# Layer 0's softmax divides the output, not the probabilities; the sums travel with the meta tokens; v's transposes later

## The chip, the cores and the metric

The kernel runs on one core of one Trainium2 chip. The metric is the time of one execution on the device in microseconds, lower is better. The kernel before took 1788.43 us (median of three runs, 1787.76 to 1789.2).

A core has five engines with a queue of instructions each: TensorE (PE, with its weight loads shown as PEld), VectorE (DVE), ScalarE (ACT), GpSimd (POOL) and SyncE (SP, which here only issues DMA transfers). Each works through its queue in order; semaphores hold an instruction until what it needs is there. Matmuls write to PSUM, a small memory that DVE and ACT read; all else lies in SBUF or in DRAM.

## The reference, cut to what matters

An encoder of two layers over 512 tokens and 16 learned meta tokens (T = 528, width 2048). Layer 0 is attention with 16 query heads of 128 on 8 pairs of key and value heads, layer 1 gated linear attention. The change lies in layer 0:

```python
def _attend(qb, k, v):
    s = jnp.einsum('bqkgd,bskd->bkgqs', qb, k) * (ATTN_HEAD_DIM ** -0.5)
    p = jax.nn.softmax(s.astype(jnp.float32), axis=-1).astype(v.dtype)
    return jnp.einsum('bkgqs,bskd->bqkgd', p, v)

def attention_mixer(h, w_in, q_norm, k_norm, w_out, ang_row, ang_col):
    proj = h @ w_in
    q, k, v, gate = jnp.split(proj, ...)
    q = apply_axial_rope(rmsnorm(q, q_norm), ang_row, ang_col)
    k = apply_axial_rope(rmsnorm(k, k_norm), ang_row, ang_col)
    ...
    return (o * jax.nn.silu(gate)) @ w_out
```

## The kernel before

**Numbers as pairs.** A float32 matrix is held as a high and a low part (names ending in h and l, or hi and lo), each in the format that PE takes for one pass. A product is three matmuls: high by high, high by low, low by high. ACT makes the high part by a copy, DVE the low part by a subtraction. Every projection of the input (`project`) is a run of 16 such triples into a PSUM tile pp, L152 to L154, once for each half of the tokens (264 columns); weights come by DMA (wraw) and are split into whi and wlo.

**Layer 0, group by group.** A group g is one pair of key and value heads with its two query heads. While a group's attention runs, PE also computes the projections of the next group (k, two of q, then v) and of gates: the attention's matmuls stand between those of the projections. The stretch of these eight groups is about 213 to 751 us of the span.

The attention of a group has nine softmaxes, eight over 128 queries and one over the 32 queries of the meta tokens. Each goes through these steps:

- scores s on PE (L636 to L638, twice three matmuls) into the only PSUM buffer of s;
- their negative maximum mx on DVE (L641);
- the exponential on ACT into the tile pn, with the row sums sm (L644);
- on DVE, the reciprocal of sm (L645), then pn times it: 512 columns of real tokens (L646), and the 16 columns of the meta tokens, written three times with 32 columns between, into the tile's tail (L647);
- transposition on PE: four transposes pT (L654) and one of the tail, pTm (L656, 80 rows);
- ACT copies pT to ph and pTm to pmt (L658, L660); DVE forms the low parts pl and the last rows of pmt (L659, L661).

The three copies in the tail stand at rows 0, 32 and 64 of pTm, against the high, low and high part of the meta tokens' v in the tile vm: one matmul does the three products. Four times in a group `weighted` follows: 13 matmuls into the PSUM tile o (L674 to L677, 256 or 272 columns), and ACT's copy of o to o_sb (L678).

**v.** v's projection is transposed as it is needed with tokens in rows. ACT copies pp to vt in two halves (L576); then PE transposes, four times vps (L581) and once vpm for the meta tokens (L588); ACT scales each part of vps by its row factor into vh (L584), DVE forms vl (L585), and likewise for vm (L590 to L592). ACT and DVE take turns here on one PSUM tile. `values` sets when the transposes are written: `clk.after(1.2, late)`, 1.2 us behind the projection by the kernel's own clock.

**PSUM.** The tiles vps, vpm, pT and pTm share a pool of two buffers (ps_t). Each new one waits until the reader of the last but one is through.

**Gates.** Stored gates come back by DMA (gr, issued on SP at L610), are multiplied on DVE (L614), go through three exponentials and logarithms on ACT (L137 to L139) and a product on POOL (gs, L624); og = o_sb times gs on DVE (L618). There are two buffers of gr, so a load waits for the product gs two gates before. POOL also rotates q and k: L294 to L296 for each of the three projections of a group (k, and q twice), on their copies qw; its inputs qs come by DMA from L293.

**What sets the order.** The program writes instructions in an order driven by a small clock (`Clock`): each triple of projection matmuls moves it by its computed length, and pieces of attention put themselves in at due times with `clk.after`. A scheduler then orders each engine's queue from priorities in that order. So a piece that is due later stands later on PE, and shifts what ACT and DVE do for it.

Of the kernel before, what the change touches and what calls it, by code (L numbers as in the profile page):

```python
# [10 lines left out]
F32 = mybir.dt.float32  # L11
F32R = mybir.dt.float32r
I32 = mybir.dt.int32
AF = mybir.ActivationFunctionType
ALU = mybir.AluOpType
# [4 lines left out]
P = 128  # L20
D = 2048
KT = D // P
SEQ = 512
META = 16
T = SEQ + META
HALF = T // 2
# [56 lines left out]
def hybrid_encoder(  # L83
# [6 lines left out]
    V, A, G, PE = nc.vector, nc.scalar, nc.gpsimd, nc.tensor  # L90
    clk = Clock()

    def pool(stack, name, bufs=1, **kw):
        return stack.enter_context(tc.tile_pool(name=name, bufs=bufs, reuse_waits="tile", **kw))
# [17 lines left out]
    ident = const.tile([P, P], F32, name="ident")  # L112
    make_identity(nc, ident)
    ones = const.tile([P, P], F32, name="ones")
# [41 lines left out]
    def project(src, c0, parts, evac, last_k=None, ws=None):  # L156

        ws = ws or [weights(src[:, k0:k0 + 8, c0:c0 + P]) for k0 in (0, 8)]
        for a, b in parts:
            ps = ps_p.tile([P, 512], F32, tag="pp", name="pp")[:, :b - a]  # L160
            for k in range(KT):
                wh, wl = ws[k // 8]
                three(ps, wh[:, k % 8], wl[:, k % 8], k, a, b, k == 0, k == KT - 1)
                clk.step(3 * (b - a + 7) / 2400)
                if last_k and (a, b) == parts[-1]:
                    last_k(k)
            evac(ps, a, b)
# [169 lines left out]
    ps_t = pool(st, "ps_t", 2, space=PSUM)  # L337
# [44 lines left out]
    for i, (si, off) in enumerate(((0, 0), (1, 0), (1, P))):  # L382
        for j, (a, b) in enumerate(HALVES):
            n = 2 * i + j
# [117 lines left out]
    ps_t = pool(ps0, "ps_t0", 2, space=PSUM)  # L502
# [56 lines left out]
    pb = pool(l0, "pb0")  # L559
    wa = pool(l0, "wa0", 2)  # L560
    NP = 3
    REP = 80
    pn_bufs = [pb.tile([P, T + 96], F32, name=f"pn{i}") for i in range(NP)]
    for t in pn_bufs:
        G.memset(t, 0.0)
    vm_bufs = [pb.tile([REP, P], F32R, name=f"vm{i}") for i in range(2)]
    for t in vm_bufs:
        G.memset(t.bitcast(F32), 0.0)
    n_pn = [0]

    def values(g):
        vh = wa.tile([P, 4, P], F32R, tag="vh", name="vh")
        vl = wa.tile([P, 4, P], F32R, tag="vl", name="vl")
        vm = vm_bufs[g % 2]
        if g:
            project(w_in0, 3072 + g * P, HALVES, lambda ps, a, b: A.copy(vt[:, a:b], ps))  # L576

        def late():
            ps = ps_t.tile([P, 512], F32, tag="t", name="vps")
            for t in range(4):  # L580
                PE.transpose(ps[:, t * P:(t + 1) * P], vt[:, t * P:(t + 1) * P], ident)  # L581
            for t in range(4):
                pst = ps[:, t * P:(t + 1) * P]
                A.activation(vh[:, t, :], pst, AF.Copy, scale=rcol[:, t:t + 1])  # L584
                V.scalar_tensor_tensor(vl[:, t, :], pst, rcol[:, t:t + 1], vh[:, t, :].bitcast(F32),  # L585
                                       op0=ALU.mult, op1=ALU.subtract)
            pm = ps_t.tile([P, 512], F32, tag="t", name="vpm")[:META, :P]
            PE.transpose(pm, vt[:, SEQ:T], ident)  # L588
            rm = rcol[:META, 4:5]
            A.activation(vm[0:META], pm, AF.Copy, scale=rm)  # L590
            A.activation(vm[64:64 + META], pm, AF.Copy, scale=rm)
            V.scalar_tensor_tensor(vm[32:32 + META], pm, rm, vm[0:META].bitcast(F32),  # L592
                                   op0=ALU.mult, op1=ALU.subtract)
        clk.after(1.2 if g else 2.0, late)
        return vh, vl, vm

    def qkv(g):
# [35 lines left out]
    def softmax(n, qh, ql, kh, kl):  # L633
        s = ps_s.tile([P, 2, 512], F32, tag="s", name="s")[:n, :, :HALF]
        for i, (a, b) in enumerate(HALVES):
            PE.matmul(s[:, i], qh, kh[:, a:b], start=True, stop=False)  # L636
            PE.matmul(s[:, i], ql, kh[:, a:b], start=False, stop=False)  # L637
            PE.matmul(s[:, i], qh, kl[:, a:b], start=False, stop=True)  # L638
        mx = wa.tile([P, 1], F32, tag="mx", name="mx")[:n]
        sm = wa.tile([P, 1], F32, tag="sm", name="sm")[:n]  # L640
        V.reduce_max(mx, s, axis=AX.XY, negate=True)  # L641
        pn = pn_bufs[n_pn[0] % NP][:n]
        n_pn[0] += 1
        A.activation(pn[:, :T].rearrange("p (a b) -> p a b", a=2), s, AF.Exp, bias=mx, accum_out=sm)  # L644
        V.reciprocal(sm, sm)  # L645
        V.tensor_scalar(pn[:, :SEQ], pn[:, :SEQ], sm, None, op0=ALU.mult)  # L646
        V.tensor_scalar(pn[:, T:].rearrange("p (r m) -> p r m", r=3)[:, :, :META],  # L647
                        pn[:, SEQ:T].unsqueeze(1).broadcast_to([n, 3, META]), sm, None, op0=ALU.mult)
        return pn

    def transposed(pn, n, puts):
        pt = ps_t.tile([P, 512], F32, tag="t", name="pT").rearrange("p (t q) -> p t q", t=4)
        for t in range(4):
            PE.transpose(pt[:, t, :n], pn[:, t * P:(t + 1) * P], ident[:n, :n])  # L654
        pm = ps_t.tile([P, 512], F32, tag="t", name="pTm")[:REP]
        PE.transpose(pm[:, :n], pn[:, T:T + REP], ident[:n, :n])  # L656
        for (ph, pl, pmt), qc, c, m in puts:
            A.copy(ph[:, :, c:c + m], pt[:, :, qc:qc + m])  # L658
            V.tensor_tensor(pl[:, :, c:c + m], pt[:, :, qc:qc + m], ph[:, :, c:c + m].bitcast(F32), op=ALU.subtract)  # L659
            A.copy(pmt[:, c:c + m], pm[:, qc:qc + m])  # L660
            V.tensor_tensor(pmt[64:, c:c + m], pm[64:, qc:qc + m], pmt[64:, c:c + m].bitcast(F32), op=ALU.subtract)  # L661

    def p_tiles():
        ph = wa.tile([P, 4, 272], F32R, tag="ph", name="ph")
        pl = wa.tile([P, 4, 272], F32R, tag="pl", name="pl")
        pmt = wa.tile([REP, 272], F32R, tag="pmt", name="pmt")
        return ph, pl, pmt

    def weighted(pts, c, n, vv, o_sb):
        ph, pl, pmt = pts  # L670
        vh, vl, vm = vv
        o = ps_o.tile([P, 512], F32, tag="o", name="o")[:, :n]
        for t in range(4):
            PE.matmul(o, vh[:, t, :], ph[:, t, :n], start=(t == 0), stop=False)  # L674
            PE.matmul(o, vh[:, t, :], pl[:, t, :n], start=False, stop=False)
            PE.matmul(o, vl[:, t, :], ph[:, t, :n], start=False, stop=False)
        PE.matmul(o, vm, pmt[:, :n], start=False, stop=True)  # L677
        A.copy(o_sb[:, c:c + n], o)  # L678

    def attention(qk, vv, o_sb, slot):  # L680
        qh, ql, kh, kl = qk
        q0 = (0, Q1)
        todo = []
        for a in range(2):
            pts = [None]
            todo += [(P, q0[a] + t * P, [(pts, 0, t * P, P)], [(pts, 0, 256, a)] if t else [], t == 0)
                     for t in range(2)]
        late = [[None], [None]]
        todo.append((2 * META, SEQ, [(late[a], a * META, 256, META) for a in range(2)], [], True))
        for a in range(2):  # L690
            todo += [(P, q0[a] + 256 + t * P, [(late[a], 0, t * P, P)], [(late[a], 256, 272, a)] if t else [], False)
                     for t in range(2)]
        prev = None
        for item in todo + [None]:
            if item is not None:
                n, c, puts, ends, fresh = item
                pn = softmax(n, qh[:, c:c + n], ql[:, c:c + n], kh, kl)
            yield slot / 2
            if prev is not None:
                n_, _, puts_, ends_, fresh_ = prev[0]  # L700
                if fresh_:
                    for cell, *_ in puts_:
                        cell[0] = p_tiles()
                transposed(prev[1], n_, [(cell[0], qc, cc, m) for cell, qc, cc, m in puts_])
                for cell, cc, m, a in ends_:
                    clk.after(slot * 1.1, lambda cell=cell, cc=cc, m=m, a=a: weighted(cell[0], cc, m, vv, o_sb[a]))
            yield slot / 2
            prev = (item, pn) if item is not None else None
        yield 0.0

    def o_tiles():
        return [wa.tile([P, T], F32, tag="o", name="o_sb", bufs=4) for _ in range(2)]

    qk, vv = qks[0][0], values(0)
    held = None
    for g in range(KV):
        o_sb = o_tiles()
# [100 lines left out]
    ps_t = pool(tr, "ps_t1", space=PSUM)  # L818
# [145 lines left out]
    for a, b in HALVES:  # L964
        ps = ps_t.tile([P, 512], F32, tag="t", name="lrf")[:64, :b - a]
        PE.matmul(ps, fold, lt[:, a:b], start=True, stop=True)
        for d in range(2):
            pd, t = ps[d * 32:d * 32 + 16], lrs[d]
# [478 lines left out]
```

## Time and profile before

| | |
|---|---|
| median of three runs | 1788.43 us |
| span of the profiled execution | 1784.8 us |
| PE busy | 1753.4 us, 98% of the span |
| DVE, ACT, POOL busy | 1126.2, 951.4, 292.8 us |
| PE busy in the stretch 205 to 755 us | 538.07 of 550 us |
| DVE, ACT busy in it | 375.88, 315.23 us |

The profile shows no time around the span; the median of the runs lies 3.6 us above it. A group's row gives a line of the kernel, the engine, the operation, what it writes and reads, and how often; then busy time, the mean time of one in ns, and the time that the engine stood idle just before it with what ended that. A row of waits names the engine and tile that waited, the instruction waited for, the total, the count and the longest. A row of the timeline begins with the start from the span's start and the duration. Matmuls overlap: the distance between starts is what one costs PE.

### The profile page before, as it was taken

Reading aid. Unit: us, or ns where it says so; the run is one execution under the profiler, and the core shown is the slowest. Engines: PE = TensorE matmul, PEld = TensorE weight load, DVE = VectorE, ACT = ScalarE, POOL = GpSimd, SP = SyncE. Lnnn points to the kernel's source line nnn. Section 1 sums busy time; section 2 is a strip of 40 time slices with the busy share of each in tenths; the row PEclk is TensorE's granted clock in tenths of the full one; section 3 lists DMA queues with packets and bytes.
Section 4 is the critical chain, followed back from the end, with each engine's and each line's share of the span. In section 5 each row is a group of like instructions: output and inputs, shape, how many; then the busy total and the mean of one; then the engine's idle time right before and its main releaser. Section 6 shows DMA issues by size and latency. Waiting matters only on the chain.

```text
span 1784.8 us, 31606 instructions
## 1 busy us (share of the span) xinstructions
PE 1753.4 (98%) x12591; PEld 1653.0 (93%) x12591; DVE 1126.2 (63%) x1883; ACT 951.4 (53%) x1912; POOL 292.8 (16%) x392
## 2 busy tenths in 40 slices
PE   8999999999999999999999999999999999999998
PEld 8999999999999999999999899988888989888886
DVE  5888776667676666722247987667684865764224
ACT  5644455556556455632347444478685765853222
POOL 3113015323423322111111001110000000000000
PEclk9999999999999999999999999999999999999999
DMA  8444423223233233343336344343332332344333
GB/s 257 139 126 134 124 78 102 85 83 107 74 96 93 76 97 104 121 117 95 96 93 195 118 141 121 99 138 88 87 108 84 103 94 86 103 144 177 95 95 130
DMA packets 265124, 200.95 MB, mean 113 GB/s; under 512 B 9772, under 2 KB 239856, under 8 KB 264448
## 3 DMA queue, kind: packets, MB, share of 16 engines
q1 hardware_dynamic: 251600, 159.00, 31.1%
q0 software_dynamic: 13376, 39.93, 6.6%
q8 instruction: 99, 1.62, 0.4%
q14 instruction: 49, 0.40, 0.1%
HBM read 164.39 MB, written 28.01 MB: 108 GB/s over the span
## 4 chain that ended last, share of the span: by engine, by line
PE 75%; ACT 2%; DVE 2%; issue 1%; DMA 0%; POOL 0%; DVEq 0%; ACTq 0%; SPq 0%
PE pp L152 15%; PE pp L154 15%; PE pp L153 15%; PE f L1359 2%; PE f L1357 2%; PE f L1358 2%; PE pp L229 2%; PE pp L231 2%; PE pp L230 2%; PE pT L654 1%; PE o L1177 1%; PE o L1178 1%; PE o L1176 1%; PE s L636 1%; PE s L637 1%; PE s L638 1%
## 5 line engine op out<-in xcount | busy, mean ns | idle before, releaser
L152 PE MATMUL pp<-uh,whi 128*128 128x264 f32 (+1 forms) x2320 | 713.4, 308 | 1.0 <-POOL whi L363 0.9
L153 PE MATMUL pp<-ul,whi 128*128 128x264 f32 (+1 forms) x2320 | 703.1, 303 | 1.5 <-DVE ul L425 1.5
L154 PE MATMUL pp<-uh,wlo 128*128 128x264 f32 (+1 forms) x2320 | 703.6, 303 | 0.3 <-POOL wlo L364 0.3
L130 DVE TENSOR_TENSOR wlo<-wraw,whi 128x1024 fp32r<-128x1024 f32 (+1 forms) x239 | 292.7, 1226 | 300.5 <-ACT whi L129 299.0
L154 PEld LDWEIGHTS pp<-uh,wlo 128*128 128x128 f32 x2320 | 438.1, 189 | 17.5 <-POOL wlo L364 0.6
L152 PEld LDWEIGHTS pp<-uh,whi 128*128 128x128 f32 x2320 | 438.1, 189 | 17.4 <-POOL whi L363 1.2
L153 PEld LDWEIGHTS pp<-ul,whi 128*128 128x128 f32 x2320 | 438.6, 189 | 15.4 <-DVE ul L425 2.0
L129 ACT CAST whi<-wraw 128x1024 fp32r<-128x1024 f32 (+1 forms) x239 | 248.8, 1042 | 294.2 <-PE pp L153 108.7
L293 POOL DMA_DIRECT2D qs<-qw x96 | 48.3, 508 | 255.9 <-ACT sq L287 219.7
L129 ACT CAST whi<-x 128x1024 fp32r<-128x1024 f32 x48 | 50.2, 1049 | 58.7 <-PE pp L230 35.9
L644 ACT ACTIVATE pn<-s,mx 128x528 f32<-128x528 f32 (+1 forms) x72 | 50.2, 697 | 50.9 <-DVE mx L641 50.9
L231 PE MATMUL pp<-uh,wlo 128*128 128x264 f32 x264 | 75.2, 285 | 0.5 <-DVE wlo L130 0.5
L1359 PE MATMUL f<-whi,ul 128*128 128x512 f32 x192 | 75.6, 394 | 0.0
L1357 PE MATMUL f<-whi,uh 128*128 128x512 f32 x192 | 75.5, 393 | 0.0
L1358 PE MATMUL f<-wlo,uh 128*128 128x512 f32 x192 | 75.3, 392 | 0.0
L229 PE MATMUL pp<-uh,whi 128*128 128x264 f32 x264 | 75.0, 284 | 0.0
L230 PE MATMUL pp<-ul,whi 128*128 128x264 f32 x264 | 74.8, 283 | 0.0
L130 DVE TENSOR_TENSOR wlo<-x,whi 128x1024 fp32r<-128x1024 f32 x48 | 60.5, 1263 | 15.7 <-ACT whi L129 15.6
L641 DVE TENSOR_REDUCE mx<-s 128x1 f32<-128x528 f32 (+1 forms) x72 | 50.6, 703 | 28.7 <-PE s L638 28.1
L659 DVE TENSOR_TENSOR pl<-pT,ph 128x512 fp32r<-128x512 f32 (+1 forms) x80 | 47.3, 592 | 17.5 <-ACT ph L658 16.7
L229 PE MATMUL pp<-th,whi 128*128 128x264 f32 x192 | 56.1, 292 | 0.8 <-ACT th L129 0.8
L658 ACT CAST ph<-pT 128x512 fp32r<-128x512 f32 (+1 forms) x80 | 40.8, 510 | 29.0 <-PE pT L654 24.6
(413 smaller groups left out, 3762.7 us busy)
## 6 DMA issues: line engine op xcount, KB each, us to landing
wraw<-in_attn_w_in_dram SPq DMA_DIRECT2D x82, 512.0 KB, 4.1
wraw<-in_gla_w_in_dram SPq DMA_DIRECT2D x81, 512.0 KB, 3.9
wraw<-in_attn_w_out_dram SPq DMA_DIRECT2D x32, 512.0 KB, 3.8
wraw<-in_gla_w_out_dram SPq DMA_DIRECT2D x32, 512.0 KB, 3.8
x<-in_gla_w_in_dram SPq DMA_DIRECT2D x15, 512.0 KB, 4.1
qs<-qw POOLq DMA_DIRECT2D x96, 66.0 KB, 3.9
x<-in_attn_w_in_dram SPq DMA_DIRECT2D x12, 512.0 KB, 4.6
x<-h_d SPq DMA_DIRECT2D x32, 132.0 KB, 3.5
```

The lines of the kernel that those rows point to most:

```text
L129: A.copy(hi, src)
L130: V.tensor_tensor(lo, src, hi.bitcast(F32), op=ALU.subtract)
L152: PE.matmul(ps, wh, uh[:, k, a:b], start=first, stop=False)
L153: PE.matmul(ps, wh, ul[:, k, a:b], start=False, stop=False)
L154: PE.matmul(ps, wl, uh[:, k, a:b], start=False, stop=last)
L229: PE.matmul(ps, w[0][:, k], bh[:, k], start=k == 0, stop=False)
L230: PE.matmul(ps, w[0][:, k], bl[:, k], start=False, stop=False)
L231: PE.matmul(ps, w[1][:, k], bh[:, k], start=False, stop=k == KH - 1)
L641: V.reduce_max(mx, s, axis=AX.XY, negate=True)
L1357: PE.matmul(ps, uh[:, k, ts], wh[:, kk], start=(k == 0), stop=False)
L1358: PE.matmul(ps, uh[:, k, ts], wl[:, kk], start=False, stop=False)
L1359: PE.matmul(ps, ul[:, k, ts], wh[:, kk], start=False, stop=(k == KT - 1))
```

## The change

The rows of pn stay undivided, and the output o is divided instead. The exponential itself writes the meta tokens' columns twice more into pn's tail (a second, small exponential, L650 in the new numbering), and the reciprocal of the row sums is written to two columns of that tail: as the tail is transposed by pTm, the reciprocals become rows 16 and 80 of pTm, and after the split into high and low parts, of pmt. A fixed matrix `sel` has ones in those two rows; the matmul `sums` = sel by pmt gives the reciprocal of each query's sum in all 128 rows. ACT copies it to o_sb, where it copied o before, and DVE multiplies o by it. Tile pn is shorter by 16 columns, pTm has 96 rows in place of 80, and sums takes its buffer from the pool ps_t.

Apart from this, v's transposes of groups 1 to 7 are due at 3.6 us behind the projection in place of 1.2.

Lines behind L562 move by 4 or more in the new kernel: vps L581 becomes L585, vl L585 L589, gr L614 L618, gs L624 L628.

```diff
--- before.py
+++ after.py
@@ -559,13 +559,17 @@
     pb = pool(l0, "pb0")
     wa = pool(l0, "wa0", 2)
     NP = 3
-    REP = 80
-    pn_bufs = [pb.tile([P, T + 96], F32, name=f"pn{i}") for i in range(NP)]
+    REP = 96
+    pn_bufs = [pb.tile([P, SEQ + 96], F32, name=f"pn{i}") for i in range(NP)]
     for t in pn_bufs:
         G.memset(t, 0.0)
     vm_bufs = [pb.tile([REP, P], F32R, name=f"vm{i}") for i in range(2)]
     for t in vm_bufs:
         G.memset(t.bitcast(F32), 0.0)
+    pick = pb.tile([REP, 1], F32, name="pick")
+    sel = pb.tile([REP, P], F32R, name="sel")
+    V.tensor_tensor(pick, ident[:REP, META:META + 1], ident[:REP, 64 + META:65 + META], op=ALU.add)
+    V.tensor_scalar(sel, ones[:REP], pick, None, op0=ALU.mult)
     n_pn = [0]
 
     def values(g):
@@ -591,7 +595,7 @@
             A.activation(vm[64:64 + META], pm, AF.Copy, scale=rm)
             V.scalar_tensor_tensor(vm[32:32 + META], pm, rm, vm[0:META].bitcast(F32),
                                    op0=ALU.mult, op1=ALU.subtract)
-        clk.after(1.2 if g else 2.0, late)
+        clk.after(3.6 if g else 2.0, late)
         return vh, vl, vm
 
     def qkv(g):
@@ -642,10 +646,9 @@
         pn = pn_bufs[n_pn[0] % NP][:n]
         n_pn[0] += 1
         A.activation(pn[:, :T].rearrange("p (a b) -> p a b", a=2), s, AF.Exp, bias=mx, accum_out=sm)
-        V.reciprocal(sm, sm)
-        V.tensor_scalar(pn[:, :SEQ], pn[:, :SEQ], sm, None, op0=ALU.mult)
-        V.tensor_scalar(pn[:, T:].rearrange("p (r m) -> p r m", r=3)[:, :, :META],
-                        pn[:, SEQ:T].unsqueeze(1).broadcast_to([n, 3, META]), sm, None, op0=ALU.mult)
+        tail = pn[:, SEQ:].rearrange("p (r m) -> p r m", r=3)
+        A.activation(tail[:, 1:, :META], s[:, 1, HALF - META:].unsqueeze(1).broadcast_to([n, 2, META]), AF.Exp, bias=mx)
+        V.reciprocal(tail[:, ::2, META], sm.broadcast_to([n, 2]))
         return pn
 
     def transposed(pn, n, puts):
@@ -653,7 +656,7 @@
         for t in range(4):
             PE.transpose(pt[:, t, :n], pn[:, t * P:(t + 1) * P], ident[:n, :n])
         pm = ps_t.tile([P, 512], F32, tag="t", name="pTm")[:REP]
-        PE.transpose(pm[:, :n], pn[:, T:T + REP], ident[:n, :n])
+        PE.transpose(pm[:, :n], pn[:, SEQ:], ident[:n, :n])
         for (ph, pl, pmt), qc, c, m in puts:
             A.copy(ph[:, :, c:c + m], pt[:, :, qc:qc + m])
             V.tensor_tensor(pl[:, :, c:c + m], pt[:, :, qc:qc + m], ph[:, :, c:c + m].bitcast(F32), op=ALU.subtract)
@@ -675,7 +678,10 @@
             PE.matmul(o, vh[:, t, :], pl[:, t, :n], start=False, stop=False)
             PE.matmul(o, vl[:, t, :], ph[:, t, :n], start=False, stop=False)
         PE.matmul(o, vm, pmt[:, :n], start=False, stop=True)
-        A.copy(o_sb[:, c:c + n], o)
+        sums = ps_t.tile([P, 512], F32, tag="t", name="sums")[:, :n]
+        PE.matmul(sums, sel, pmt[:, :n], start=True, stop=True)
+        A.copy(o_sb[:, c:c + n], sums)
+        V.tensor_tensor(o_sb[:, c:c + n], o, o_sb[:, c:c + n], op=ALU.mult)
 
     def attention(qk, vv, o_sb, slot):
         qh, ql, kh, kl = qk
```

How the queues move is shown at three places, all at the start of group 3. On PE, around v's transposes: pp are the next group's projection, s the scores, vps and vpm v's transposes, pT and pTm those of the first softmax. Before:

```order
L154 MATMUL pp<-uh,wlo 128x264
L581 MATMUL vps<-ident,vt 128x128 x4
L588 MATMUL vpm<-ident,vt 16x128
L152 MATMUL pp<-uh,whi 128x264
...
L654 MATMUL pT<-ident,pn_2505 128x128 x4
L656 MATMUL pTm<-ident,pn_2505 80x128
```

After:

```order
L585 MATMUL vps<-ident,vt 128x128 x4
L592 MATMUL vpm<-ident,vt 16x128
L152 MATMUL pp<-uh,whi 128x264
L153 MATMUL pp<-ul,whi 128x264
L154 MATMUL pp<-uh,wlo 128x264
L640 MATMUL s<-kh_2487,qh_2489 128x264
...
L657 MATMUL pT<-ident,pn_2505 128x128 x4
L152 MATMUL pp<-uh,whi 128x264
L153 MATMUL pp<-ul,whi 128x264
L154 MATMUL pp<-uh,wlo 128x264
L659 MATMUL pTm<-ident,pn_2505 96x128
```

Between the last matmul of o and vps stand now 60 projection matmuls and sums, where 39 stood. Behind vpm came 24 projection matmuls, six of s and 15 more, then pT and pTm; now three, six of s and 15 more, then pT, three and pTm.

On DVE, around the four vl: mx is a softmax's maximum, gr the second gate, ql, sl and wlo low parts. Before:

```order
L585 SCALAR_TENSOR_TENSOR vl<-vps,rcol,vh 128x128
L130 TENSOR_TENSOR ql_2490<-qw_96,qh_2489 128x512
L130 TENSOR_TENSOR ql_2490<-qw_96,qh_2489 128x16
L614 TENSOR_TENSOR gr<-gr,rrow 128x528
L645 RECIPROCAL sm<-sm 128x1
L585 SCALAR_TENSOR_TENSOR vl<-vps,rcol,vh 128x128
L646 TENSOR_SCALAR pn_2505<-pn_2505,sm 128x512
L647 TENSOR_SCALAR pn_2505<-pn_2505,sm 128x3x16
L585 SCALAR_TENSOR_TENSOR vl<-vps,rcol,vh 128x128
L592 SCALAR_TENSOR_TENSOR vm_2512<-vpm,rcol,vm_2512 16x128
L641 TENSOR_REDUCE mx<-s 128x1
L585 SCALAR_TENSOR_TENSOR vl<-vps,rcol,vh 128x128
```

After:

```order
L651 RECIPROCAL pn_2505<-sm 128x2
L589 SCALAR_TENSOR_TENSOR vl<-vps,rcol,vh 128x128
L596 SCALAR_TENSOR_TENSOR vm_2512<-vpm,rcol,vm_2512 16x128
L589 SCALAR_TENSOR_TENSOR vl<-vps,rcol,vh 128x128
L645 TENSOR_REDUCE mx<-s 128x1
L589 SCALAR_TENSOR_TENSOR vl<-vps,rcol,vh 128x128
L618 TENSOR_TENSOR gr<-gr,rrow 128x528
L651 RECIPROCAL pn_2506<-sm 128x2
L589 SCALAR_TENSOR_TENSOR vl<-vps,rcol,vh 128x128
L662 TENSOR_TENSOR pl<-pT,ph 128x4x128
```

The second gate's gr and the reciprocal of the second softmax stand now between the third and the fourth vl; gr stood between the first and the second.

On POOL, where group 2 ends: og_d is the store of a gated output, gs the product of a gate (L624, then L628), the rest the last rotation of the group. Before:

```order
L619 DMA og_d<-o_sb 128x528
L624 TENSOR_TENSOR gs<-gs,gr 128x528
L294 TENSOR_TENSOR qw_96<-qw_96,cos 128x528
L295 TENSOR_TENSOR qs<-qs,sin 128x528
L296 TENSOR_TENSOR qw_96<-qw_96,qs 128x528
```

After:

```order
L623 DMA og_d<-o_sb 128x528
L294 TENSOR_TENSOR qw_96<-qw_96,cos 128x528
L295 TENSOR_TENSOR qs<-qs,sin 128x528
L628 TENSOR_TENSOR gs<-gs,gr 128x528
L296 TENSOR_TENSOR qw_96<-qw_96,qs 128x528
```

gs moved behind two of the rotation's products, here and at the ends of groups 3 and 4; at the end of group 1 it stays behind all three.

## The prediction

> **What bounds the kernel now.** I read the page's first table, then the engine waits of the stretch 205 to 755 us (layer 0's attention, where the change lies), then the granted clock by windows, then the timeline where the longest waits are. The page first:
>
> ```profile
> span 1784.8 us, 31606 instructions
> PE 1753.4 (98%) x12591; PEld 1653.0 (93%) x12591; DVE 1126.2 (63%) x1883; ACT 951.4 (53%) x1912; POOL 292.8 (16%) x392
> ```
>
> PE is the bound; DVE works 63% of the span. Work taken from DVE therefore counts only where PE waits for it, and work given to PE counts in full. Where PE waits in the stretch (us in total, times, longest):
>
> ```profile
> PE vps L581 <- ACT vt L576: 5.1, 4, 3.2
> PE vps L581 <- DVE pl L659: 2.3, 1, 2.3
> PE pT L654 <- DVE pl L659: 2.2, 2, 2.1
> PE s L636 <- ACT qh L129: 1.6, 1, 1.6
> PE s L637 <- DVE ql L130: 0.3, 1, 0.3
> ```
>
> Most of it is v's transposition (vps) at the start of a group. It waits for ACT's copy vt of v's projection 5.1 us in four groups, and 2.3 us in group 1 for a PSUM buffer. The longest of these also costs clock (windows around 356.86; columns PE, PEld, DVE, ACT, POOL with counts, then granted clock):
>
> ```profile
> 353.60:356.80 3.20, 0.10 (x1) 0.00 (x0) 2.62 (x5) 2.70 (x7) 0.58 (x1) 0.83 0.56 152
> 356.80:360.00 3.20, 3.14 (x15) 3.07 (x16) 2.80 (x9) 3.16 (x10) 0.00 (x0) 0.50 0.45 151
> 360.00:363.00 3.00, 3.00 (x17) 3.00 (x17) 0.90 (x3) 0.97 (x3) 1.30 (x1) 0.58 0.45 116
> 363.00:366.00 3.00, 3.00 (x27) 3.00 (x27) 1.50 (x4) 1.58 (x5) 0.00 (x0) 1.00 0.22 78
> ```
>
> After 3.2 us without work the clock is 0.50 to 0.58 for 6.2 us. 15 + 17 = 32 matmuls ran there; at the later rate of 27 in 3 us they take 3.6 us, so 2.6 us were lost. The waits that the change aims at cost 5.1 + 2.3 + 2.6 = 10.0 us.
>
> **PE's new work.** The 32 matmuls of sums are as wide as the last one of o (256 or 272 columns). What one costs is the distance between starts:
>
> ```profile
> 352.94 0.29 PE L152 MATMUL pp<-uh,whi 128*128 128x264 f32 x1
> 353.07 0.28 PE L153 MATMUL pp<-ul,whi 128*128 128x264 f32 x1
> 353.19 0.29 PE L154 MATMUL pp<-uh,wlo 128*128 128x264 f32 x1
> ```
>
> 353.19 - 352.94 over two is 0.12 us; 32 x 0.12 = 3.9 us, on the path, since PE is the bound. The transpose pTm has 96 rows of output in place of 80 and the same moving width: nothing.
>
> **DVE and ACT.** The groups of instructions (columns: busy us, mean ns):
>
> ```profile
> L646 DVE TENSOR_SCALAR pn<-pn,sm 128x512 f32<-128x512 f32 x64 | 34.7, 542 | 1.9
> L647 DVE TENSOR_SCALAR pn<-pn,sm 128x48 f32<-128x48 f32 x64 | 25.3, 396 | 0.0
> L310 DVE SCALAR_TENSOR_TENSOR sq<-ssq,erow 128x264 f32<-128x264 f32 x42 | 18.1, 430 | 11.4 <-PE ssq L308 10.7
> L660 ACT CAST pmt<-pTm 80x16 fp32r<-80x16 f32 x16 | 2.7, 170 | 0.0
> L591 ACT ACTIVATE vm<-vpm,rcol 16x128 fp32r<-16x128 f32 x8 | 2.9, 358 | 0.1
> ```
>
> DVE loses 34.7 + 25.3 = 60.0 us (a little more with the eight small softmaxes) and gains 32 products o times sums, from PSUM with one operand in SBUF like L310: 32 x 0.43 = 13.8 us. All of it lies beside PE. ACT gains 72 exponentials of 2 x 16 columns; none stands in the trace, so it is bounded by L660's 0.17 us and L591's 0.36 us: 72 x 0.25 = 18 us, also beside PE. The copy of o becomes a copy of sums of the same size. The tail exponential reads s, so the one buffer of s comes free some 0.25 us later; scores stand about 2 us of PE work and more behind it, so nothing.
>
> The DVE pair also stretches at one place where PE waits behind it:
>
> ```profile
> 292.44 1.37 DVE L646 TENSOR_SCALAR pn<-pn,sm 128x512 f32<-128x512 f32 x1
> 293.73 1.31 DVE L647 TENSOR_SCALAR pn<-pn,sm 128x48 f32<-128x48 f32 x1
> 300.12 0.39 PE L636 MATMUL s<-kh,qh 128*128 128x264 f32 x1 [1.64 <-ACT qh L129]
> ```
>
> Both go, and with them up to 2.7 us ahead of wlo, the norm and qh on DVE's queue. The score matmul seven microseconds later is not wholly behind them, so I take 1.0 us off (bounds 0 and 1.9, the whole wait).
>
> **Buffers.** sums takes one of two PSUM buffers that vps, vpm, pT and pTm share; its matmul waits for pl of the pT before it, and a pTm after it waits for ACT's copy.
>
> ```profile
> 432.83 0.60 PE L654 MATMUL pT<-ident,pn 128*128 128x128 f32 x4
> 434.42 0.69 DVE L659 TENSOR_TENSOR pl<-pT,ph 128x512 fp32r<-128x512 f32 x1 [0.28 <-ACT ph L658]
> ```
>
> pl ends 2.3 us after that pT began, and sums stands 2.3 to 2.5 us of PE work behind its pT: 0 to 1 us over all groups, 0.5 taken.
>
> **v's transposes, later.** Group 3 shows them best (start, duration):
>
> ```profile
> 416.08 1.31 POOL L624 TENSOR_TENSOR gs<-gs,gr 128x528 f32<-128x528 f32 x1 [1.56 <-ACT gs L139]
> 417.36 1.32 POOL L294 TENSOR_TENSOR qw<-qw,cos 128x528 f32<-128x528 f32 x1
> 420.05 1.33 POOL L296 TENSOR_TENSOR qw<-qw,qs 128x528 f32<-128x528 f32 x1
> ...
> 417.42 0.34 SPq L610 DMA_DIRECT2D gr<-g_d  x1
> ...
> 419.97 0.29 PE L677 MATMUL o<-pmt,vm 80*128 80x272 f32 x1
> ...
> 420.21 1.73 DVE L614 TENSOR_TENSOR gr<-gr,rrow 128x528 f32<-128x528 f32 x1 [3.53 <-DMA gr<-g_d]
> ...
> 424.02 0.65 ACT L139 ACTIVATE gs<-gs 128x528 f32<-128x528 f32 x1
> 426.58 0.36 ACT L576 COPY vt<-pp 128x264 f32<-128x264 f32 x1
> ...
> 426.99 0.44 PE L581 MATMUL vps<-ident,vt 128*128 128x128 f32 x2 [0.76 <-ACT vt L576]
> ...
> 432.35 0.34 DVE L585 SCALAR_TENSOR_TENSOR vl<-vps,rcol,vh 128x128 fp32r<-128x128 f32 x1
> ...
> 433.27 0.27 PE L656 MATMUL pTm<-ident,pn 128*80 128x128 f32 x1
> ```
>
> Let e be the start of the last matmul of o, 419.97. vt starts at e + 6.6. PE had 5.9 us of work from there to vps, and waited. The new order has 21 more projection matmuls and one of sums there (22 x 0.12 = 2.7 us), so that vps comes at e + 8.6: the wait for vt goes, and 10.0 us with it, if vt keeps its place. What is late next is the end of the same chain. pTm needs the PSUM buffer that the last vl releases; in group 3 that was 432.69, 5.7 us after 426.99. Before, pTm stood 433.27 - 426.99 = 6.3 us behind vps, which covered it. In the new order 5 transposes of v, 21 projection and 6 score matmuls and 4 of pT stand between, 36 in all, about 4.3 us. The cover is gone and PE waits.
>
> How long follows from two queues. The fourth vh on ACT now stands behind the second softmax's exponential, whose scores follow vps by 1.7 us; with mx 0.7, the exponential 0.9 and vh and vl 0.35 each that is 4.6 us with the hand-overs: a wait of at least 0.3 us. In groups 2 to 4 DVE's queue has, between the third and the fourth vl, the second gate's product gr, which waits for its DMA. That is issued when POOL's gs has read the old buffer, and gs follows ACT's L139, which now stands behind vt and the first softmax's exponential and tail: vt 0.36, exponential 0.9, tail 0.25, L139 0.65, gs 1.31, the load 2.8 (417.42 to 420.21), gr 0.7, vl 0.35. That is e + 6.6 + 7.3 = e + 13.9, against pTm at e + 8.6 + 4.3 = e + 12.9: a wait of about 1.2 us with a hand-over.
>
> At the start of groups 3 to 5, POOL's order has the last gate's gs behind the two products L294 and L295 (first below), so the first gr is loaded some 3.5 us later. DVE's queue waits for it ahead of the o products and the norm, and so does vt behind them: e + 10. Then vps waits about 1.8 us again, and pTm, by the same sum, 2.7 us: 4.5 us in groups 3 and 4, and in 5, without gr between, less. This is the dear case.
>
> Per group I take: group 1, where vps and then sums wait for vl and pl, 1.9 (1.5 to 2.3, the old wait); group 2, 2.0 (0.6 to 3.2); groups 3 and 4, 2.4 each (1.2 to 4.5), nearer the low end, because DVE's queue is shorter by 0.7 us a softmax and the load has room in it; group 5, 1.6 (0.6 to 3.2); group 6, 0.9 (0.3 to 0.9); group 7, 0. Together 11.2 us (5.4 to 18.6). The wait of pT for pl in the last group, 2.1 us, has no other work before it and stays.
>
> **The sum.** 3.9 (sums) + 0.5 (buffers) - 1.0 (scores at 300 us) - 10.0 (old waits) + 11.2 (new waits) = +4.6 us: a span of 1789.4 us. The median of the runs, 1788.43, is 3.6 us over the profiled span, and I carry that over: 1793.0 us. The ends are 3.9 + 0 - 1.9 - 10.0 + 5.4 = -2.6 and 3.9 + 1 - 0 - 10.0 + 18.6 = +13.5.
>
> On the clock, the idle time in group 1 stands beside that of group 2:
>
> ```profile
> 231.00:234.00 3.00, 0.75 (x7) 0.67 (x7) 2.51 (x6) 0.89 (x3) 0.00 (x0) 1.00 0.25 70
> 234.00:237.00 3.00, 3.00 (x27) 3.00 (x26) 2.21 (x6) 2.39 (x7) 0.00 (x0) 1.00 0.37 112
> ```
>
> 2.3 us without work left it at 1.00, 3.2 us did not; new waits of 1 to 2.7 us should leave it. The Trainium skill, "TensorE: Matmul & The Clock Gate", section "🔬 Part 1: The HAM clock gate (the "warmup" mystery)", has the clock halved after an idle window of about 3.4 us and whole again after about 3.4 us of work. The two rows agree with the first part; by the second the loss would be an estimated 1.7 us in place of 2.6, and the sum +5.5.
>
> **Rivals.**
> A: the waits go and none comes back. DVE is 46 us lighter in the stretch, so vt and vl move ahead by what DVE held them up, and pTm finds its buffer free. For it: PE's new order covers vt as it stood. Against it: 5.7 us of chain behind vps under 4.3 us of work. With 1.5 us left of new waits: 3.9 - 1.0 - 10.0 + 1.5 = -5.6, 1782.8 us. It decides if the last vl ends within 4.3 us of vps in most groups. Chance 0.22.
> B: a balance. The chain keeps the length of group 3's trace, so pTm waits 5.7 - 4.3 = 1.4 us at most and about 1.0 on average in six groups, and group 1 keeps 1.5: 7.5 us. 3.9 + 0.5 - 1.0 - 10.0 + 7.5 = +0.9, 1789.3 us. For it: POOL's order is on no chain that the trace shows as PE's wait. Chance 0.27.
> C: the dear case, and clock with it. In groups 3 and 4 vps and pTm wait 4.5 us within 6 us. If the clock falls there as at 356.80, 2 x 2.6 = 5.2 us come on top: 1798.2 us. Against it: the 2.3 us at 231 us cost none. Chance 0.10.
> The Trainium skill, same page, section "A second HAM failure mode: psum-queue depth-cycling", lets frequent short idles from PSUM buffers change the clock to and fro; sums and pTm in two buffers would be such idles, C's mechanism in every group. The row at 234 us speaks against it, as far as one wait can.
>
> **How the numbers follow.** Forecast 0.41, A 0.22, B 0.27, C 0.10. A measurement of this kernel can tell about 0.2%, 3.6 us, from no change. A is faster with most of its chance, and so is a little of B and of the forecast's low end: 0.27. B and the forecast's low part lie within: 0.30. The rest, with C, is slower: 0.43. The forecast's own range is 1785.8 to 1802; with A it begins at 1783, and at 1801 little of C is left out.
>
> **What would show it.** Right: the waits of PE name pTm or vm's buffer <- DVE vl for 5 us or more in total, vps <- ACT vt is below 2 us, PE's busy time is 3.9 us longer, and the window behind 356 us has a clock of 1.00. Wrong: vl ends inside 4.3 us of vps (A); vps waits for vt in groups 3 to 6 by 1.5 us and more each (the dear case); or sums itself waits for pl by more than 1 us in total.

## The result, and the profile after

The changed kernel takes 1800.65 us (median of four runs, 1796.8 to 1803.7) against 1788.1 us: a ratio of 1.0065, with a 95% interval from 1.0044 to 1.0085. It is slower, as forecast, but by 12.5 us between the medians (11.6 by the ratio) where 4.6 were forecast.

The profiled execution of the changed kernel is the fastest of the four (1796.8 us). Its first table shows what the change moved: DVE is 49 us lighter, PE 7.4 us heavier.

```profile
span 1795.1 us, 31685 instructions
PE 1760.8 (98%) x12623; PEld 1657.4 (92%) x12623; DVE 1076.8 (60%) x1773; ACT 964.4 (54%) x1984; POOL 291.8 (16%) x392
```

The waits of PE in the stretch 205 to 770 us answer to those of before:

```profile
PE pTm L659 <- DVE vl L589: 6.0, 4, 2.7
PE s L640 <- ACT pn L650: 3.1, 2, 2.2
PE sums L682 <- DVE pl L662: 3.1, 6, 2.0
PE s L640 <- ACT qh L129: 0.8, 1, 0.8
PE pT L657 <- DVE vm L596: 0.5, 1, 0.5
```

vps, which waited 5.1 us for vt and 2.3 us for pl, is gone from the list. pTm waits for the last vl in its place, 6.0 us in four groups. New are the waits of the scores for the tail exponential (L650), of sums for pl, and of pT for vm. Of sums' 3.1 us, 2.0 are the last group's wait, which stood at pT before.

The longest of pTm's waits is in group 4, at 503.8 us, and the half clock follows it (windows; the last three columns are clock, DMA share and GB/s):

```profile
503.80:506.50 2.70, 0.01 (x1) 0.00 (x0) 1.06 (x4) 1.49 (x5) 0.00 (x0) 0.95 0.16 63
506.50:509.50 3.00, 2.97 (x14) 2.97 (x15) 0.86 (x2) 0.26 (x1) 0.00 (x0) 0.50 0.00 0
```

14 matmuls in 3 us, where 27 run at full clock: 13 x 0.11 = 1.4 us lost, against 2.6 us behind 356 us in the kernel before.

What holds the last vl, the timeline of group 3 shows (SP, POOL, ACT, DVE and PE):

```profile
429.61 1.32 POOL L628 TENSOR_TENSOR gs<-gs,gr 128x528 f32<-128x528 f32 x1 [4.79 <-ACT gs L139]
...
430.95 0.34 SPq L614 DMA_DIRECT2D gr<-g_d  x1
...
432.49 0.36 ACT L588 ACTIVATE vh<-vps,rcol 128x128 fp32r<-128x128 f32 x1
...
431.68 0.34 DVE L589 SCALAR_TENSOR_TENSOR vl<-vps,rcol,vh 128x128 fp32r<-128x128 f32 x1
434.07 0.71 DVE L618 TENSOR_TENSOR gr<-gr,rrow 128x528 f32<-128x528 f32 x1 [2.05 <-DMA gr<-g_d]
434.77 0.33 DVE L589 SCALAR_TENSOR_TENSOR vl<-vps,rcol,vh 128x128 fp32r<-128x128 f32 x1
...
435.16 0.31 PE L659 MATMUL pTm<-ident,pn 128*96 128x128 f32 x1 [2.07 <-DVE vl L589]
```

The fourth vh is ready at 432.85, and vl needs nothing else. But DVE has the second gate's product gr ahead of it, idles 2.05 us for gr's load, and starts the last vl at 434.77. The load was issued at 430.95, as soon as POOL's gs had read the old buffer.

The first matmul of the output projection (po) tells how much of this lies in the stretch, before and after:

```profile
749.97 0.28 PE L152 MATMUL po<-uh,whi 128*128 128x264 f32 x1
...
762.01 0.28 PE L152 MATMUL po<-uh,whi 128*128 128x264 f32 x1
```

The profiled execution has lost 12.0 us by then, 0.7 of them before 205 us. From there on PE's order is the same in both kernels, 6645 matmuls long, and 1.8 us come back, so that the spans differ by 10.3 us.

The mean granted clock of the four runs falls as their time grows: 0.998 in the profiled one, 0.996 at 1798.84 us, 0.995 at 1802.46 and at 1803.7 us.

### The profile page after: what moved, and what is told of

Its sections match the earlier page's. It is cut to its first block, busy times and chain, and to the rows that moved or that the text cites. A ratio compares the mean times of both kernels' runs of the same rounds, so it can differ in the third digit from the quotient of the medians.

```text
span 1795.1 us, 31685 instructions
## 1 busy us (share of the span) xinstructions
PE 1760.8 (98%) x12623; PEld 1657.4 (92%) x12623; DVE 1076.8 (60%) x1773; ACT 964.4 (54%) x1984; POOL 291.8 (16%) x392
## 4 chain that ended last, share of the span: by engine, by line
PE 57%; DVE 3%; ACT 1%; issue 1%; DMA 0%; POOL 0%; DVEq 0%; ACTq 0%; SPq 0%
PE pp L152 11%; PE pp L154 10%; PE pp L153 10%; PE f L1365 2%; PE f L1363 2%; PE f L1364 2%; PE pp L229 2%; PE pp L231 2%; PE pp L230 2%; PE o L1183 1%; PE o L1184 1%; PE o L1182 1%; PE pp L1365 1%; PE pp L1363 1%; PE pp L1364 1%
## 5 line engine op out<-in xcount | busy, mean ns | idle before, releaser
L230 PE MATMUL pp<-tl,whi 128*128 128x264 f32 x192 | 54.4, 284 | 0.0
```

The source lines that it names most:

```text
L230: PE.matmul(ps, w[0][:, k], bl[:, k], start=False, stop=False)
```

## The experiments

All are timed against the kernel before, 1788.6 to 1789.0 us on the chips of these runs, with 95% intervals of the ratio. First each half of the change alone.

**1. v's transposes later, nothing else.**

```diff
-        clk.after(1.2 if g else 2.0, late)
+        clk.after(3.6 if g else 2.0, late)
```

> The kernel before with v's transposes of groups 1 to 7 due at 3.6 us in place of 1.2, nothing else of the change. Theory (the divided output costs 3.9 us of sums on PE and its buffers, and v's lateness trades the wait for vt against a wait of pTm for the last vl): vps waits for vt no more (-5.1 us and -2.6 us of clock), pTm waits for vl by 1 to 6 us in all; 1782 to 1788 us against 1788. Rival A (v's lateness by itself is the loss): 1795 to 1802 us. Rival B (the lateness is a clear gain, and the divided output alone loses about 20 us): below 1781 us.

Measured: 1790.8 us, 1.0011 (1.0001 to 1.0022). PE's waits:

```profile
PE pTm L656 <- DVE vl L585: 6.6, 5, 3.1
...
PE vps L581 <- ACT vt L576: 1.0, 1, 1.0
```

The trade is there as said, but at a worse rate: 6.6 us of waits for vl where 1 to 6 were expected, and 1.0 us of the wait for vt stays. The time lies above the 1782 to 1788 us expected, and below rival A's. Moving the transposes alone gains nothing.

**2. The divided output, transposes at 1.2 us as before.**

```diff
-        clk.after(3.6 if g else 2.0, late)
+        clk.after(1.2 if g else 2.0, late)
```

> The changed kernel with v's transposes due at 1.2 us as before. Theory: vt comes 8 us behind o's last matmul in groups 3 to 5 and vps stands at 6, so vps waits 2 to 3 us in three or four groups and the clock falls in one or two, while pTm waits for vl no more: as slow as the change, 1797 to 1804 us. Rival A (the lateness is the loss): 1788 to 1792 us.

Measured: 1799.8 us, 1.0059 (1.0047 to 1.0071), as slow as the whole change.

```profile
PE vps L585 <- ACT vt L580: 8.1, 4, 2.6
PE sums L682 <- DVE pl L662: 3.1, 6, 2.0
```

vt is later than in the kernel before (8.1 us of waiting against 5.1), and pTm doesn't wait at all. So the divided output costs 10 to 11 us wherever the transposes stand (the change against experiment 1, and this one against the kernel before); their place only chooses who waits. Rival A falls.

**3. The divided output without sums.** The matmul, its copy and the product are left out, so the output lacks the division.

```diff
-        sums = ps_t.tile([P, 512], F32, tag="t", name="sums")[:, :n]
-        PE.matmul(sums, sel, pmt[:, :n], start=True, stop=True)
-        A.copy(o_sb[:, c:c + n], sums)
-        V.tensor_tensor(o_sb[:, c:c + n], o, o_sb[:, c:c + n], op=ALU.mult)
+        A.copy(o_sb[:, c:c + n], o)
```

> The changed kernel without the matmul of sums and without the product by it: o is copied undivided as before, so the output lacks the division. Theory: PE's 3.9 us and the 3.1 us for which sums waits for pl go: 1792 to 1794.5 us against 1800.7. Rival A: only PE's 3.9 us go, 1796 to 1798 us.

Measured: 1785.85 us, 0.9981 (0.9972 to 0.999): 14.8 us below the change, where 6 to 9 were expected.

```profile
PE pTm L659 <- DVE vl L589: 3.1, 2, 2.9
PE s L640 <- ACT pn L650: 2.2, 3, 1.2
PE pT L657 <- DVE pl L662: 2.0, 1, 2.0
```

With sums went half of pTm's wait: in groups 3 and 4 gr stands ahead of the four vl (in the kernel before it stood behind the first), and POOL's gs ahead of the rotation again. So something in the division reaches the gates.

**4. A third buffer for gr.**

```diff
-        grs = [wa.tile([P, T], F32, tag="gr", name="gr") for _ in hs]
+        grs = [wa.tile([P, T], F32, tag="gr", name="gr", bufs=3) for _ in hs]
...
-                gr = wa.tile([P, T], F32, tag="gr", name="gr", bufs=2)
+                gr = wa.tile([P, T], F32, tag="gr", name="gr", bufs=3)
...
-    sel = pb.tile([REP, P], F32R, name="sel")
+    sel = ones[:REP].bitcast(F32R)
```

The tile of ones is filled anew behind the layer.

> The changed kernel with three buffers of gr in place of two, sel kept in the tile of ones to make room; the order of every queue is the same. Theory: the last vl stands behind the second gate's gr, which waits for its load; with a third buffer the load starts a gate earlier, pTm's wait for vl falls from 6.0 to below 1.5 us and with it the half clock behind the longest: 1791 to 1796 us against 1800.7. Rival (pTm waits because ACT and DVE take turns over vh and vl): pTm's wait stays above 4 us, 1799 to 1802 us.

Measured: 1798.6 us, 1.0048 (1.0036 to 1.006). pTm's wait went in group 2 and stayed in groups 3 and 4:

```profile
PE pTm L659 <- DVE vl L589: 4.1, 2, 2.4
...
431.89 0.34 SPq L614 DMA_DIRECT2D gr<-g_d  x1
...
434.78 0.71 DVE L618 TENSOR_TENSOR gr<-gr,rrow 128x528 f32<-128x528 f32 x1 [1.76 <-DMA gr<-g_d]
```

This experiment missed its aim. The loads ran one gate ahead, and so did the products on DVE: the product between the third and the fourth vl is now that of the next gate, and it waits for a load issued at 431.89, again behind POOL's gs. Its numbers lie nearer the rival's, but they don't decide for it: the extra buffer moved the queue along, not the wait out of it.

**5. The matmul of sums without the product.** o is copied undivided and nobody reads sums, so the output lacks the division.

```diff
-        A.copy(o_sb[:, c:c + n], sums)
-        V.tensor_tensor(o_sb[:, c:c + n], o, o_sb[:, c:c + n], op=ALU.mult)
+        A.copy(o_sb[:, c:c + n], o)
```

> The changed kernel with the matmul of sums in its place and buffer, but without the product: o is copied undivided and sums is read by nobody, so the output lacks the division. Theory (sums costs PE its 3.9 us and, in the shared buffers, small waits for pl and refills that the trace of the change adds up to some 5 us; the product costs the rest by its delay of the gates): between 1793 and 1796 us, 8 to 9 us over the kernel without sums at 1785.9. Rival A (only PE's work counts): 1789 to 1791 us. Rival B (the product's delay is all that is left, buffers are free): also 1790, with no wait of sums for pl above 0.3 us in total but the last group's.

Measured: 1791.9 us, 1.0021 (1.0011 to 1.0031), between the two expectations. It parts the 14.8 us of experiment 3: 6.0 us are the matmul in its buffer (3.9 of work, some 2 net of waits and late starts), 8.8 us come with the product and with the copy that now waits for sums. The second part is known to some 4 us only, as the change's four runs spread over 7 us. The profiled execution is the longest of this experiment's twelve (1799.18 us), so no trace shows where the 8.8 us lie.

**6. sums in the projections' buffers.**

```diff
-        sums = ps_t.tile([P, 512], F32, tag="t", name="sums")[:, :n]
+        sums = ps_p.tile([P, 512], F32, tag="pp", name="sums")[:, :n]
```

> The changed kernel with sums in the three buffers of the projections in place of the two that pT, pTm and v's transposes share. POOL's order at the ends of groups 2 to 4 comes back to that of the kernel before. Theory: sums waits for pl no more (-3.1 us and some 2 us of refills), the first gate comes earlier: 1792 to 1796 us against 1800.7. Rival (the buffers don't matter): 1799 to 1802 us.

Measured: 1792.9 us, 1.002 (1.0012 to 1.0029), 7.8 us below the change.

```profile
PE pTm L659 <- DVE vl L589: 3.9, 3, 1.5
...
PE pT L657 <- DVE pl L662: 2.0, 1, 2.0
...
PE pp L152 <- ACT o_sb L683: 1.4, 1, 1.4
```

sums waits no more, and pTm's longest wait is 1.5 us: the first gate is earlier, since POOL's gs stands ahead of the rotation again. A projection now waits once for the copy.

**7. gr's product on POOL.** This takes the waiting instruction out of DVE's queue and leaves PE's order as it is, matmul for matmul.

```diff
-            V.tensor_tensor(gr, gr, rrow, op=ALU.mult)
+            G.tensor_tensor(gr, gr, rrow, op=ALU.mult)
```

> The changed kernel with the product gr by rrow of the stored gates on POOL in place of DVE; PE's order is the same. Theory: the last vl no longer stands behind a product that waits for its load, so pTm waits for vl by less than 1.5 us in place of 6.0, and no half clock follows: 1793 to 1797 us against 1800.7. Rival (the turns of ACT and DVE over vh and vl are too long anyway): pTm still waits over 4 us, 1799 to 1802 us.

Measured: 1788.6 us, 0.9994 (0.9985 to 1.0002): 12.1 us below the change, where 4 to 8 were expected, and no slower than the kernel before. PE's waits, and group 3 on POOL and DVE:

```profile
PE sums L682 <- DVE pl L662: 3.1, 6, 2.0
PE s L640 <- ACT pn L650: 2.6, 2, 2.3
PE s L640 <- ACT qh L129: 0.6, 1, 0.6
...
430.48 1.31 POOL L618 TENSOR_TENSOR gr<-gr,rrow 128x528 f32<-128x528 f32 x1 [3.11 <-DMA gr<-g_d]
...
429.83 0.34 DVE L589 SCALAR_TENSOR_TENSOR vl<-vps,rcol,vh 128x128 fp32r<-128x128 f32 x1
431.03 0.35 DVE L589 SCALAR_TENSOR_TENSOR vl<-vps,rcol,vh 128x128 fp32r<-128x128 f32 x1
...
426.90 0.60 PE L585 MATMUL vps<-ident,vt 128*128 128x128 f32 x4
431.44 0.31 PE L659 MATMUL pTm<-ident,pn 128*96 128x128 f32 x1
```

The wait for the load is still there, 3.11 us, but POOL spends it. The last vl ends at 431.38, 4.5 us behind vps, and pTm, 4.5 us behind vps by its own order, doesn't wait. It is the place of the product, not DVE's relief: DVE is busy 1070.8 us against 1076.8 in the change, and in experiment 10 1126.9 us against 1126.2. How much of the 12.1 us belongs to the change, experiment 10 shows.

**8. The tail by a copy from pn**, not by a second exponential.

```diff
-        A.activation(tail[:, 1:, :META], s[:, 1, HALF - META:].unsqueeze(1).broadcast_to([n, 2, META]), AF.Exp, bias=mx)
+        V.tensor_copy(tail[:, 1:, :META], pn[:, SEQ:T].unsqueeze(1).broadcast_to([n, 2, META]))
```

> The changed kernel with the tail of pn written by a DVE copy from pn in place of the second exponential of s. Theory: the scores wait for the tail (3.1 us in two places) only for its 0.28 us and the hand-over each, the rest is the first exponential's own lateness: 1799 to 1801 us, scores wait for ACT's exponential by 1.5 to 2.7 us. Rival (the tail exponential holds s and costs all of the wait): 1796 to 1798 us.

Measured: 1798.9 us, 1.0052 (1.004 to 1.0064).

```profile
PE s L640 <- ACT pn L648: 2.5, 2, 2.0
```

The time lies just under the theory's range, and the waits decide for it: the scores wait 2.5 us for the first exponential where they waited 3.1 for the second. In these two executions the tail's own part is about 0.6 us; the rest is the first exponential, late anyway.

**9 to 12. The repairs together, and on the kernel before.** 9 has the edits of 6 and 7; 10 is the kernel before with the edit of 7; 11 is that of experiment 1 with the edit of 7; 12 is 9 with the transposes at 2.4 us.

> The changed kernel with both: gr by rrow on POOL and sums in the projections' buffers. Theory (the two waits are separate): 1784.5 to 1787.5 us, below the 1788.6 of the first alone by the 1.1 us of sums' waits outside the last group and some refills. Rival (the gain of the other buffer was that of the earlier gate alone, and is had already): 1788 to 1790 us.

> The kernel before with gr by rrow on POOL and nothing else: a control. Theory: there DVE's product gr stands ahead of the norm and so of vt, and its wait for the load adds to vps' wait for vt (5.1 us and 2.6 us of clock in the trace); some of it goes: 1782 to 1787 us. Rival (gr on POOL repairs only what the change broke): 1788 to 1790 us.

> The kernel before with v's transposes at 3.6 us and gr by rrow on POOL, the probabilities still divided. Theory: vps waits no more for vt, and pTm's wait for vl falls from 6.6 to below 3 us: 1782 to 1786 us, as good as or better than the changed kernel with the same repair, since that one pays 3.9 us for sums. Rival (the lighter DVE is what makes the repair work): 1788 to 1791 us.

> The changed kernel with gr by rrow on POOL, sums in the projections' buffers and v's transposes at 2.4 us. Theory: with gr out of DVE's queue neither vt nor vl is late, so 2.4 or 3.6 makes little difference: within 2 us of the same kernel at 3.6. Rival (vt still comes 8 us behind o): vps waits for vt 2 us and more in total, 2 to 5 us slower than at 3.6.

| | us | ratio to before, interval |
|---|---|---|
| 9: change, gr on POOL, sums in other buffers | 1786.7 | 0.9988 (0.9979 to 0.9997) |
| 10: before, gr on POOL | 1784.8 | 0.9979 (0.997 to 0.9987) |
| 11: before, transposes at 3.6, gr on POOL | 1786.0 | 0.998 (0.9972 to 0.9989) |
| 12: as 9, transposes at 2.4 | 1786.6 | 0.9989 (0.998 to 0.9998) |

All four times came as the theory had them. Two of the waits did not: pTm's in 11 is 4.7 us, longer than the 3 expected, and in 10 vps still waits 5.1 us in total for vt, as in the kernel before. What went in 10 is the longest of these waits, 1.3 us in place of 3.2, and the half clock behind it (1.00 in the window 356.60 to 359.60 us). The profiled execution of 10 is the longest of its eleven, so where the rest of the gain lies isn't shown.

10 has the lowest median, 4.2 us under the kernel before; 11 is 1.2 us above it. So of the 12.1 us of experiment 7 some 4 can be had without the change, and about 8 are what the change itself lost at gr (known to some 4 us, by the spread of the change's runs). With gr out of DVE's queue the change costs 1788.6 - 1784.8 = 3.8 us. That this is near the 3.9 us of its matmuls is chance: it is a net of matmuls, buffers and old waits, and with sums in other buffers and the same matmuls it is 1786.7 - 1784.8 = 1.9 us. The place of the transposes no longer matters beyond 1.2 us (10 and 11; 9 and 12).

## Why the prediction was right, and where its sizes were off

**The mechanism held.** The wait for vt went and a wait of pTm for the last vl came, behind the second gate's product and its load. Experiment 7 shows it: this one instruction on another queue, PE's order the same, and these waits are gone. The chain for group 3, a wait of about 1.2 us, measured 2.07: vt came at e + 7.7 in place of e + 6.6, and the rest of the chain followed it.

**The number was partly luck.** The forecast was 1793.0 us; 1800.65 lies just inside the upper end of its range. Several terms were off, and not all the same way. In the profiled execution the stretch lost 11.3 us (12.0 less the 0.7 before 205 us) where the sum had 4.6. One of the signs that it gave for being wrong came, too: sums waits for pl by more than 1 us in total, 3.1 with the last group's wait and 1.1 without. And PE's busy time grew by 7.4 us, not by 3.9.

**The old waits**, 10.0 us, went in full. **The wait at 300 us** (-1.0) shrank by 0.8. **The new waits** of v's transposition, put at 11.2, came to 7.9: pTm 6.0, pT for vm 0.5, clock 1.4. **The scores**, for which the prediction had "nothing", wait 3.1 us; experiment 8 puts this on the first exponential more than on the tail.

**POOL's order** was read rightly and its effect too strongly. Group 3 in the changed kernel, the last matmul of o and vt's copy:

```profile
420.07 0.29 PE L680 MATMUL o<-pmt,vm 96*128 96x272 f32 x1
...
427.75 0.37 ACT L580 COPY vt<-pp 128x264 f32<-128x264 f32 x1
```

vt came at e + 7.7, not e + 10, and vps at its e + 8.6 didn't wait.

**The buffers**, put at 0.5 us, were the term of the sum most underrated. The prediction took the time from a pT to the end of its pl from one place, 2.3 us. At this place, in group 2, it is longer:

```profile
406.57 0.60 PE L657 MATMUL pT<-ident,pn 128*128 128x128 f32 x4
...
410.34 0.68 DVE L662 TENSOR_TENSOR pl<-pT,ph 128x512 fp32r<-128x512 f32 x1
...
411.08 0.39 PE L682 MATMUL sums<-pmt,sel 96*128 96x272 f32 x1 [0.20 <-DVE pl L662]
```

pl ends 4.5 us behind pT, since ACT and DVE have parts of the weights and of q to form first, and PE reaches sums before that. What the table of waits doesn't count is seen at the next such place:

```profile
480.89 0.28 PE L152 MATMUL pp<-uh,whi 128*128 128x264 f32 x1
481.40 0.39 PE L682 MATMUL sums<-pmt,sel 96*128 96x272 f32 x1 [0.23 <-DVE pl L662]
481.63 0.29 PE L153 MATMUL pp<-ul,whi 128*128 128x264 f32 x1
```

sums starts 0.51 us behind the matmul ahead of it and the next one 0.23 us behind sums, where 0.12 each is usual: 0.5 us are lost, and 0.23 stand in the row. Read in this way over all 32 sums, 15 of them lose 7.0 us; 2.3 of these are the last group's, which pT had before, so about 4.7 are new. In the trace of experiment 6 sums loses nothing. Experiment 5 has less, 2.1 us beside the work of the matmul, but that is a net of all that moved; and with gr on POOL the other buffers bring only 1.9 us (9 against 7). What became of the rest there is not shown.

Put together from the trace: 3.9 (sums) + 4.7 (buffers) - 0.8 (scores at 300 us) - 10.0 (old waits) + 7.9 (new waits) + 3.1 (scores) = 8.8 of the stretch's 11.3 us. The other 2.5 us were not parted.

**The product's delay of the gates.** I had counted its 13.8 us on DVE as lying beside PE. They do, but the kernel without the product is 8.8 us faster (experiment 5 against the change), and with neither product nor sums gr stands elsewhere around vl (experiment 3). That the product acts through o_sb, gs and the load of gr fits this, and is argued, not shown step by step. Nor is it a term to be added to the sum above: the waits of pTm and their clock are part of it. DVE's relief bought little: in experiment 3 DVE is 58 us lighter than in experiment 1, and the time about 5.0 us shorter.

**On the clock**, the prediction took 2.3 us without work for harmless, from one row. Behind 356 us the clock was whole, as it said, but a wait of 2.7 us in group 4 brought half the clock. The spread of the change's four runs, 7 us, goes with it: an estimate from their granted clocks, 0.995 against 0.998 over 1800 us, is 5.4 us, and the two runs at 0.995 are 5.7 and 6.9 us longer than the profiled one. PE's waits of 2 to 2.7 us are just those that sometimes cost the clock (last section). That these runs lose it behind these waits is likely, and not shown, as no trace of them is kept.

Rival B, a balance at 1789.3 us, had the new waits better than the forecast (7.5 us, against 7.9 measured), and failed on the buffers and the scores, as the forecast did. Rival A failed on the last vl, as its condition said. Rival C, at 1798.2 us and a chance of 0.10, came nearest to the measured time, but not by its mechanism: its half clock came in group 4 alone, and vps, which was to wait there as well, did not.

## What to carry to other kernels

Before an engine that isn't the bound is relieved, look at what its queue holds in front of the few instructions for which the bound waits: here 49 us of relief were worth less than the place of one 0.7 us product that waits for a load (some 8 us of this change, and 4 of the kernel before). If an instruction waits for a DMA, put it on the engine for which nobody waits; an added buffer may only let the next one take its place. And a matmul that is added where PE is the bound costs its full time, with its buffer's waits on top (6.0 us for 3.9 us of work in experiment 5), however much work it takes from others.

## What the runs showed of the hardware

The granted clock doesn't follow the length of an idle stretch alone. Windows just behind a wait of PE, in order: 2.3 us (the scores' in experiment 7, at 228 us), 2.4 us (pTm's in experiment 4, group 4), 2.6 us (vps' in experiment 2, group 4) and 2.9 us (pTm's in experiment 3, group 2):

```profile
228.70:231.70 3.00, 2.99 (x13) 2.99 (x14) 2.62 (x4) 1.41 (x3) 1.56 (x2) 0.50 0.63 188
...
507.00:510.00 3.00, 3.00 (x19) 3.00 (x20) 0.82 (x2) 0.26 (x1) 0.00 (x0) 0.71 0.00 0
...
503.00:506.00 3.00, 3.00 (x26) 2.98 (x26) 2.21 (x7) 2.54 (x9) 0.72 (x1) 1.00 0.46 131
...
364.35:367.35 3.00, 3.00 (x25) 3.00 (x26) 0.93 (x3) 0.26 (x1) 0.00 (x0) 1.00 0.00 0
```

The shortest was followed by half the clock, the longest by none of it. The Trainium skill, "TensorE: Matmul & The Clock Gate", section "🔬 Part 1: The HAM clock gate (the "warmup" mystery)", puts the half clock behind an idle window of about 3.4 us and has that window run freely, not set anew when a kernel starts. These rows agree with a window that runs freely, as a longer wait can leave the clock whole where a shorter one does not. They do not agree with 3.4 us as the idle time that it takes: every wait here is shorter.
